# DeltaNet heads of a hybrid layer: low parts of weights and scaled value rows taken off GpSimd

## The chip, the cores and the metric

The kernel runs on one core of a Trainium2 chip, as one launch. The metric is the device time of that launch in microseconds (us), as the median of several runs; the profile is that of one more execution, whose own time stands in the table below. The engines are TensorE (PE in the profile, PEld for its weight loads), VectorE (DVE), ScalarE (ACT), GpSimd (POOL) and SyncE (SP). Each runs its own queue in order.

## What is computed

One layer for 1152 tokens (128 of context, 1024 latent) and a model width of 1024. From one normalised and modulated input h one combined projection gives q, k, v and z of four DeltaNet heads, decay and beta, the input u of a pooling mixer, and two gates. Both branches are projected, merged by the gates, projected again, and a SwiGLU layer follows. The part that the change touches, cut from the reference:

```python
def _layer(x, cvec, s0, grid_w, ...):
    h = _rmsnorm(x, g_pre_mix) * (1.0 + sc1) + sh1
    qkv, z, a, b, u, gate_a, gate_b = _split_cols(h @ w_in)
    qkv = _short_conv(qkv, conv_w)
    y_a, s_fin = _delta_branch(qkv, z, a, b, s0, a_log, dt_bias, g_onorm)
    y_b = _pool_branch(u, w_pool, pool_scale, grid_w)
    merged = jax.nn.sigmoid(gate_a) * (y_a @ w_a_proj) + jax.nn.sigmoid(gate_b) * (y_b @ w_b_proj)
...
def _gated_delta_chunked(q, k, v, g, beta, s0):
...
    t_inv = lax.linalg.triangular_solve(eye + lower, ...)
    u = jnp.einsum('nbhij,nbhjv->nbhiv', t_inv, vc * bc[..., None])
...
    def step(S, inp):
        v_new = u_i - jnp.einsum('bhck,bhkv->bhcv', w_i, S)
        o_i = jnp.einsum('bhck,bhkv->bhcv', qd_i, S) + jnp.einsum('bhij,bhjv->bhiv', intra_i, v_new)
        S = S * jnp.exp(gl_i)[..., None, None] + jnp.einsum('bhck,bhcv->bhkv', kd_i, v_new)
```

## The kernel before

**Matmuls in split form.** Each large matrix product is made of three matmuls: weight and activation are split into a high part, rounded by a copy of ACT, and a low part, source minus high part, by a `tensor_tensor` of another engine. `gemm` issues high by high (L517), high weight by low activation (L518) and low weight by high activation (L519) for each of three column chunks of 384 tokens. A weight tile comes by DMA (`wraw`); `w_split` makes `whi` (ACT, L168) and `wlo` (L169) from it, two buffers each. It is called by `w_ahead` when the first chunk of the GEMM before has done two of its steps, so the split of a weight is issued one GEMM ahead of its use. Which engine makes `wlo` stands in `lo_eng[0]`: DVE at first, POOL from the point in `gemm_stream` after the first head's q, k and v, DVE again for the layer's output projection.

**Scaled outputs.** `scaled` multiplies a PSUM result by a column, in turn on ACT (L204) and on DVE (L207, L209), and splits the product: high part on ACT (L212), low part (L214) on DVE in even turns and on `lo_alt[0]` in odd ones. `lo_alt[0]` is DVE until the normalised input is done, and POOL after it; the odd turns after it are six in `pool_proj` (the pooling mixer's group product, four groups `g` by three chunks) and four near 1003 us, in a later norm.

**The heads.** `delta_head` runs the four heads one after the other, each for both directions of the scan. Its serial chain goes: transposes of k and q (L845); products of k by k and k by q (`gk`, L873), which DVE multiplies with decay and beta into `W` and `D` (L878, L881); blocks of `W` to DRAM and back, so that 72 blocks of 32x32 stand on 72 partitions; the substitution, 31 steps of two DVE instructions each (L909 a product, L911 a sum); the result `XB` to DRAM and back as `XS` and `X`; a DVE transpose of `XS` (L952); the small matmuls `l1a` (L967) and their like, which put the 32x32 inverses together to 128x128; then nine steps of the recurrence. A `step` is PE `p1` (L1083), DVE `rr` (L1087), PE `p2` (L1097), DVE `v2` (L1102), PE `p3` (L1118), DVE `S` (L1126), with ACT's `v1` and `ou` (L1108, L1111) and the output sums `oa` (L1060, L1062, and L1064 on POOL) beside it.

**Value rows.** In the steps 14, 16 and 18 of the substitution, three blocks of v are transposed by PE into PSUM, copied to `vT` by ACT (L926) and multiplied in place by a column per block, `nk`, the reciprocal norm of k, on POOL (L927): 12 copies and 12 products in four heads.

**Order.** The program's order is written out by hand: between the serial steps the calls `fill(ns)` draw from the generator `gemm_stream` as much GEMM work (z, gates, and q, k, v of the next head) as the number asks for. All that a GEMM step issues, the weight split included, goes into the queues at that place, so an ACT copy or a low part stands between whichever rows of the serial chain were issued before and after it.

Of the kernel before, what the change touches and what calls it, by code (L numbers as in the profile page):

```python
# [12 lines left out]
AF = mybir.ActivationFunctionType  # L13
ALU = mybir.AluOpType
# [3 lines left out]
P = 128  # L18
# [5 lines left out]
CH = 384  # L24
# [55 lines left out]
def hybrid_layer(ctx: ExitStack, tc: tile.TileContext, ins, outs, dbg=None):  # L80
    nc = tc.nc
    PE, DVE, ACT, POOL, SP = nc.tensor, nc.vector, nc.scalar, nc.gpsimd, nc.sync
# [17 lines left out]
    def slot(dtype=F32, name="s"):  # L100
        uid[0] += 1
        return slots.tile([P, SL], dtype, tag="s", name=f"{name}{uid[0]}")
# [7 lines left out]
    def psd(name="d"):  # L110
        if given:
            return given.pop(0)
        uid[0] += 1
        return ps.tile([P, 512], F32, tag="d", bufs=5, name=f"{name}{uid[0]}")
# [5 lines left out]
    def v3(ap, a, b, o=0):  # L120
        return ap[:, o:o + a * b].rearrange("p (a b) -> p a b", b=b)
# [4 lines left out]
    def bc_last(ap, n):  # L126
        return ap.rearrange("p (n o) -> p n o", o=1).to_broadcast([ap.shape[0], ap.shape[1], n])
# [5 lines left out]
    lo_eng, w_dma = [DVE], [SP]  # L133
# [60 lines left out]
    lo_alt = [DVE]  # L194
# [23 lines left out]
    def sqrt_cols(x, n, inverse):  # L218

        s = small([P, 16], "rs1", 2)[:, 0:n]  # L220
        r = small([P, 16], "rs2", 2)[:, 0:n]
        a = small([P, 16], "rs3", 2)[:, 0:n]
        y = small([P, 16], "rs4", 6)[:, 0:n]
        ACT.activation(out=s, in_=x, func=AF.Sqrt)
        DVE.reciprocal(out=r, in_=s)
        DVE.tensor_tensor(out=a, in0=r, in1=r, op=ALU.mult)
        DVE.tensor_tensor(out=a, in0=a, in1=x, op=ALU.mult)
        DVE.tensor_scalar(out=a, in0=a, scalar1=-0.5, scalar2=1.5, op0=ALU.mult, op1=ALU.add)
        DVE.tensor_tensor(out=y, in0=r, in1=a, op=ALU.mult)
        if not inverse:  # L230
            z = small([P, 16], "rs5", 6)[:, 0:n]
            DVE.tensor_tensor(out=z, in0=y, in1=x, op=ALU.mult)
            return z
        return y
# [15 lines left out]
    with tc.manual_schedule():  # L250
# [112 lines left out]
        pt = psd("cs")  # L363
# [141 lines left out]
        def flush_bg():  # L505
            while bg:
                bg.popleft()()
# [65 lines left out]
        def silu_pending(n=12):  # L573
            while silus and n:
                t = silus.popleft()
                ACT.activation(out=t[:, 0:1154], in_=t[:, 0:1154], func=AF.Silu)
                n -= 1
# [91 lines left out]
        def u_task(g, early=None):  # L669
            u = slot(name="u")  # L670

            def evac(c, o):
                ACT.copy(out=u[:, c * CH:(c + 1) * CH], in_=o)

            if early is None:
                yield from gemm(8, h_at, evac)
            else:
                w, acc = early
                for c, o in enumerate(acc):
                    evac(c, o)  # L680
                w_ahead()
                w_more()
                if len(acc) < NCH:
                    yield from gemm(8, h_at, evac, w=w, chunks=range(len(acc), NCH))
            pool_group(g, u)
# [4 lines left out]
        def ab_task():  # L690

            abt.append(slot(name="ab"))
            hl, _ = w_get()
            for c in range(NCH):
                o = psg()[0:32, 0:CH]
                for k in range(8):
                    w = hl[:, k * 32:(k + 1) * 32]
                    for i, a in enumerate(h_at(k, c)):
                        PE.matmul(o, w, a, start=(k + i == 0), stop=(k + i == 8))
                    if k == 1:  # L700
                        if c == 0:
                            w_ahead()
                        elif c == 1:
                            w_more()
                    bg_tick()
                    yield 350
                ACT.copy(out=abt[0][0:32, c * CH:(c + 1) * CH], in_=o)
# [114 lines left out]
        def delta_head(h, fill, prev_final):  # L822
            def tk(t, c):
                o = tokpos(c * P)
                return t[:, o:o + P]
# [17 lines left out]
            for c in range(NT):  # L843
                pt = psd("tr")
# [26 lines left out]
            for c in range(NT):  # L871
                pt = psd("gk")
# [3 lines left out]
                cs = slice(c * P, (c + 1) * P)  # L876
                for d in range(2):
                    DVE.scalar_tensor_tensor(out=W[d][:, cs], in0=pt[:, 0:P], scalar=bn[d][:, c:c + 1],  # L878
                                             in1=IN[d][:, cs], op0=ALU.mult, op1=ALU.mult)
# [15 lines left out]
            nk = sqrt_cols(ske, NT, False)  # L895
# [6 lines left out]
            vT = slot(name="vT")  # L902
# [3 lines left out]
            for s in range(31):  # L906
                n, m = 31 - s, s + 1
                o = tt[0:72, 0:n * m].rearrange("p (r c) -> p r c", c=m)
                DVE.tensor_tensor(out=o, in0=wb[:, s + 1:32, s:s + 1].to_broadcast([72, n, m]),  # L909
                                  in1=xb[:, s:s + 1, 0:m].to_broadcast([72, n, m]), op=ALU.mult)  # L910
                DVE.tensor_tensor(out=xb[:, s + 1:32, 0:m], in0=xb[:, s + 1:32, 0:m], in1=o, op=ALU.add)  # L911
                fill(F_SUB)
                if s == 8:
                    next(prev_final, None)
                    until(f"v{h}")
                    flush_bg()
                    silu_pending()
                    vC = qkvC.pop(h)[2]
                if s in (14, 16, 18):

                    c = 3 * (s // 2 - 7)
                    cs = slice(c * P, (c + 3) * P)
                    pt = psd("tv")
                    for i in range(3):
                        PE.transpose(pt[:, i * P:(i + 1) * P], tk(vC, c + i), ident)
                    ACT.copy(out=vT[:, cs], in_=pt[:, 0:CH])  # L926
                    POOL.tensor_tensor(out=v3(vT, 3, P, c * P), in0=v3(vT, 3, P, c * P), in1=bc_last(nk[:, c:c + 3], P),  # L927
                                       op=ALU.mult)
            SP.dma_start(out=sx_d.rearrange("d c b r s -> (d c b) (r s)"), in_=XB[0:72, 0:1024])
            X = [slot(name="X") for _ in range(2)]  # L930
            Xv = [v3(x, NT, P) for x in X]
# [357 lines left out]
        def mod_ahead():  # L1289
            tiles = mod_buf.pop() if mod_buf else [slot(name="wm") for _ in range(4)]  # L1290
            mod_q.append(mod_load(*MODS[mod_i[0]], tiles))
            mod_i[0] += 1

        def mod_end():
            while mod_late:
                mod_late.pop()()
# [25 lines left out]
        def with_mod(task, ahead=True):  # L1322
            yield from task
            mod_end()
            mod_step()
            if ahead:
                mod_ahead()
            else:
                mod_buf.clear()
            yield 3000  # L1330

        def mark(name):
            done.add(name)
            return
            yield
# [3 lines left out]
        def gemm_stream():  # L1339
            mod_ahead()  # L1340
            yield from u_task(GORD[0], early[0])
            yield from u_task(GORD[1], early[1])
            for g in GORD[2:]:
                yield from with_mod(u_task(g))
            yield from with_mod(ab_task())
            yield from qkv_tasks(0, lambda t, j: with_mod(t, j < 2))
            lo_eng[0] = POOL
            yield from mark("qkv0")
            yield from pool_proj()
            mod_end()  # L1350
            for m in range(8):
                yield from yb_task(m)
            yield from mark("yb")
            for h in range(H):
                yield from z_task(h)
                yield from mark(f"z{h}")
                for i, (kind, m) in enumerate(GATES[h]):
                    if i == N_FIRST and h + 1 < H:
                        yield from qkv_tasks(h + 1)
                    if m == 7 and kind == "a":  # L1360
                        for k in range(H - 1):
                            ya_load(k)
                    yield from (ga_task if kind == "a" else gb_task)(m)
            flush_bg()
            for m in range(8):
                yield from pre_task(m)
            yield from mark("end")
# [5 lines left out]
        def fill(ns):  # L1373
            debt[0] += ns
            while debt[0] > 0 and "end" not in done:
                if stopped[0] in done:
                    debt[0] = 0.0
                    return
                x = next(stream, None)
                if x is None:  # L1380
                    break
                debt[0] -= x

        def until(name):
            while name not in done:
                next(stream, None)
# [54 lines left out]
        norm_end()  # L1441
        for i in range(len(units) - lag, len(units)):
            early_mm(*units[i])
        lo_alt[0] = POOL
        xt = None
        until("qkv0")
        fill(4000)
# [797 lines left out]
        for s, key in enumerate(keys[:-4]):  # L2245
            i, j = key[0]
# [73 lines left out]
```

## Time and profile before

| | |
|---|---|
| median of 3 runs | 1778.08 us (1776.79 to 1781.83) |
| profiled execution, its own time | 1779.98 us |
| its span | 1778.2 us |
| mean granted clock of TensorE | 0.974 of full |
| busy: PE, DVE, ACT, POOL | 1670.6, 1135.0, 712.5, 565.4 us |

The span is the time from the first to the last recorded instruction of the profiled execution; the 1.8 us between it and the execution's own time lie around it. The granted clock is the share of full speed that TensorE was allowed. DVE, ACT and POOL are busy less than two thirds of the span, so what their work costs depends on where PE waits for it.

### The profile page before, as it was taken

The page shows a single profiled execution, that of the slowest core. Times are in us where ns is not written, and L with a number is a line of the kernel's source. Part 1 is how long each engine was busy: PE and PEld are TensorE (multiplying, and loading weights), DVE is VectorE, ACT ScalarE, POOL GpSimd, SP SyncE. Part 2 cuts the span into 40 slices and gives each one's busy share as a digit, 9 for nine tenths or more (in the row PEclk, how much of TensorE's full clock was granted, in tenths as well). Part 3 has the DMA queues.
Part 4 walks back from the last instruction along what each step waited for, and adds up shares of the span by engine and source line. Part 5 has one row for each costly group of instructions (what it writes and reads, how often), then busy time and mean ns, then how long its engine had stood idle before and what let it go on. Part 6 is the DMA issues. An engine that isn't in the chain of part 4 may idle for free.

```text
span 1778.2 us, 26020 instructions
## 1 busy us (share of the span) xinstructions
PE 1670.6 (94%) x10103; PEld 1526.3 (86%) x10103; DVE 1135.0 (64%) x2067; ACT 712.5 (40%) x1381; POOL 565.4 (32%) x438
## 2 busy tenths in 40 slices
PE   5999999899999899898897799999999999899998
PEld 3977998889999889888676799999999999678776
DVE  4697546669468469457568655555555555467797
ACT  4414552463362362232356533323333333243553
POOL 0001212423333242145201456666666663000000
PEclk8999999999999899998999899999999999999999
DMA  9354432223314213453352122222222223853344
GB/s 325 99 174 156 147 113 82 67 54 114 90 32 128 57 51 122 129 203 115 107 210 98 60 92 92 93 92 92 81 79 77 84 84 113 293 203 95 126 157 172
DMA packets 173388, 211.61 MB, mean 119 GB/s; under 512 B 34956, under 2 KB 118373, under 8 KB 173265
## 3 DMA queue, kind: packets, MB, share of 16 engines
q1 hardware_dynamic: 139180, 178.35, 30.3%
q10 hardware_dynamic: 31205, 19.80, 3.8%
q0 software_dynamic: 2880, 11.80, 1.8%
q8 instruction: 79, 1.29, 0.3%
q14 instruction: 44, 0.36, 0.1%
HBM read 159.99 MB, written 49.93 MB: 118 GB/s over the span
## 4 chain that ended last, share of the span: by engine, by line
PE 46%; DVE 12%; ACT 4%; DMA 3%; issue 3%; POOL 2%; SPq 0%; DVEq 0%; ACTq 0%; POOLq 0%
PE m L1818 5%; PE m L1817 5%; PE m L1816 5%; PE dn L2160 3%; PE dn L2159 3%; PE c L1863 3%; PE dn L2158 3%; PE c L1862 3%; PE c L1861 3%; DVE WD L909 2%; PE g L517 2%; PE g L518 1%; PE g L519 1%; DVE XB L911 1%; DVE ulo L191 1%
## 5 line engine op out<-in xcount | busy, mean ns | idle before, releaser
L517 PE MATMUL g<-hh,whi 128*128 128x384 f32 x824 | 300.0, 364 | 2.8 <-ACT sga L1253 2.7
L519 PE MATMUL g<-hh,wlo 128*128 128x384 f32 x824 | 279.9, 340 | 0.0
L518 PE MATMUL g<-hl,whi 128*128 128x384 f32 x824 | 278.2, 338 | 0.0
L169 POOL TENSOR_TENSOR wlo<-wraw,whi 128x1024 fp32r<-128x1024 f32 (+2 forms) x42 | 86.3, 2055 | 280.0 <-ACT whi L168 243.6
L191 DVE TENSOR_TENSOR ulo<-wsum,uhi 128x1024 fp32r<-128x1024 f32 (+1 forms) x56 | 99.8, 1783 | 104.6 <-ACT uhi L190 104.6
L517 PEld LDWEIGHTS g<-hh,whi 128*128 128x128 f32 x824 | 156.4, 190 | 9.7 <-ACT sga L1253 3.4
L518 PEld LDWEIGHTS g<-hl,whi 128*128 128x128 f32 x824 | 157.1, 191 | 0.0
L519 PEld LDWEIGHTS g<-hh,wlo 128*128 128x128 f32 x824 | 156.0, 189 | 0.0
L1863 PE MATMUL c<-h3h,ulo 128*128 128x384 f32 x352 | 119.6, 340 | 2.7 <-DVE ulo L191 2.7
L1862 PE MATMUL c<-h3l,uhi 128*128 128x384 f32 x352 | 119.4, 339 | 0.0
L1861 PE MATMUL c<-h3h,uhi 128*128 128x384 f32 x352 | 119.2, 339 | 0.0
L1745 POOL TENSOR_TENSOR wsum<-wr,wr 128x512 f32<-128x512 f32 x63 | 101.9, 1638 | 47.8 <-DMA wr<-in_w_up_dram 43.4
L191 DVE TENSOR_TENSOR ulo<-wr,uhi 128x512 fp32r<-128x512 f32 x92 | 94.2, 1063 | 32.6 <-ACT uhi L190 32.6
L190 ACT ACTIVATE uhi<-wsum 128x1024 fp32r<-128x1024 f32 (+1 forms) x56 | 57.4, 1025 | 134.2 <-PE c L1862 50.3
L1816 PE MATMUL m<-oah,uhi 128*128 128x384 f32 x260 | 88.6, 341 | 5.7 <-ACT sgu L1828 5.7
L1745 POOL TENSOR_TENSOR wsum<-wr 128x512 f32<-128x512 f32 x43 | 58.1, 1359 | 102.5 <-DVE wlo L169 93.5
L1816 PE MATMUL m<-obh,uhi 128*128 128x384 f32 x260 | 88.8, 341 | 1.4 <-ACT uhi L190 1.4
L1818 PE MATMUL m<-obh,ulo 128*128 128x384 f32 x260 | 88.9, 342 | 0.7 <-DVE ulo L191 0.7
L2158 PE MATMUL dn<-wdhi,fh 128*128 128x512 f32 x216 | 85.8, 397 | 3.1 <-ACT fh L190 3.1
L1818 PE MATMUL m<-oah,ulo 128*128 128x384 f32 x260 | 88.6, 341 | 0.0
L1817 PE MATMUL m<-oal,uhi 128*128 128x384 f32 x260 | 88.4, 340 | 0.0
L1817 PE MATMUL m<-obl,uhi 128*128 128x384 f32 x260 | 88.4, 340 | 0.0
(448 smaller groups left out, 4419.7 us busy)
## 6 DMA issues: line engine op xcount, KB each, us to landing
wm<-in_w_mod_dram SPq DMA_DIRECT2D x48, 512.0 KB
wr<-in_w_up_dram SPq DMA_DIRECT2D x44, 512.0 KB
fr<-fo_d SPq DMA_DIRECT2D x35, 512.0 KB
wraw<-in_w_in_dram ACTq DMA_DIRECT2D x26, 512.0 KB
fo_d<-fs SPq DMA_DIRECT2D x22, 512.0 KB
wd<-in_w_down_dram SPq DMA_DIRECT2D x44, 256.0 KB
wraw<-in_w_o_dram SPq DMA_DIRECT2D x20, 512.0 KB
fo_d<-sgu SPq DMA_DIRECT2D x11, 512.0 KB
```

The source lines that it names most:

```text
L191: eng.tensor_tensor(out=lo, in0=src, in1=hi.bitcast(F32), op=ALU.subtract)
L517: PE.matmul(o, wh, a_hi, start=(k == 0), stop=False)
L518: PE.matmul(o, wh, a_lo, start=False, stop=False)
L519: PE.matmul(o, wl, a_hi, start=False, stop=(k == nk - 1))
L1745: eng.tensor_tensor(out=v3(s, 4, P, 512 * i), in0=w_block(u, a), in1=w_block(u, b), op=op)
L1816: PE.matmul(o, wh[:, ks], bh, start=(kp == 0), stop=False)
L1817: PE.matmul(o, wh[:, ks], bl, start=False, stop=False)
L1818: PE.matmul(o, wl[:, ks], bh, start=False, stop=(kp == 3))
L1861: PE.matmul(o, wh[:, ks], bh, start=(k == 0), stop=False)
L1862: PE.matmul(o, wh[:, ks], bl, start=False, stop=False)
L1863: PE.matmul(o, wl[:, ks], bh, start=False, stop=(k == 7))
L2158: PE.matmul(o, fh[:, fs], wh[:, w], start=(j == 0), stop=False)
```

## The change

Two assignments go, so that `lo_eng[0]` and `lo_alt[0]` stay DVE for the heads and `pool_proj`; and the copy and product of `vT` become three ACT activations with a scale column, one per block.

```diff
@@ delta_head, substitution, steps 14, 16 and 18
                     for i in range(3):
                         PE.transpose(pt[:, i * P:(i + 1) * P], tk(vC, c + i), ident)
-                    ACT.copy(out=vT[:, cs], in_=pt[:, 0:CH])
-                    POOL.tensor_tensor(out=v3(vT, 3, P, c * P), in0=v3(vT, 3, P, c * P), in1=bc_last(nk[:, c:c + 3], P),
-                                       op=ALU.mult)
+                    for i in range(3):
+                        ACT.activation(out=vT[:, (c + i) * P:(c + i + 1) * P], in_=pt[:, i * P:(i + 1) * P], func=AF.Copy,
+                                       scale=nk[:, c + i:c + i + 1])
@@ gemm_stream
             yield from qkv_tasks(0, lambda t, j: with_mod(t, j < 2))
-            lo_eng[0] = POOL
             yield from mark("qkv0")
             yield from pool_proj()
@@ after the normalised input
             early_mm(*units[i])
-        lo_alt[0] = POOL
         xt = None
         until("qkv0")
```

52 low parts change their engine from POOL to DVE: 42 of weights (29 of 128x1024, 8 of 128x512, 5 of 128x384) and 10 of scaled outputs (128x384). Their place in the program does not change; that of DVE's rows does, since each now stands in DVE's queue. PE's order is the same.

The first place is DVE's queue at the beginning of `pool_proj`. `ybl` and `ybh` are low and high part of an output, `sp` the scaled output itself, `wlo` a weight's low part; a row ahead of the first of these is the copy L399. Lines with + are new on DVE.

```order
+L169 TENSOR_TENSOR wlo_1508<-wraw_1329,whi_1507 128x512
+L214 TENSOR_TENSOR ybl_1514<-sp_1519,ybh_1513 128x384
 L209 TENSOR_SCALAR sp_1527<-g_1523,vcol 128x384
 L214 TENSOR_TENSOR ybl_1514<-sp_1527,ybh_1513 128x384
+L214 TENSOR_TENSOR ybl_1514<-sp_1535,ybh_1513 128x384
 L209 TENSOR_SCALAR sp_1545<-g_1541,vcol 128x384
 L214 TENSOR_TENSOR ybl_1540<-sp_1545,ybh_1539 128x384
+L214 TENSOR_TENSOR ybl_1540<-sp_1553,ybh_1539 128x384
 L209 TENSOR_SCALAR sp_1561<-g_1557,vcol 128x384
```

Between two scalings `sp` of DVE there stood one low part; now there are two, and the first of them belongs to the output that ACT has scaled.

The second place is DVE's queue in the substitution of head 0, in its second half.

```order
 L909 TENSOR_TENSOR WD_2350<-WB_2361,XB_2362 72x220
 L911 TENSOR_TENSOR XB_2362<-XB_2362,WD_2350 72x10x22
+L169 TENSOR_TENSOR wlo_2649<-wraw_2438,whi_2648 128x1024
 L909 TENSOR_TENSOR WD_2350<-WB_2361,XB_2362 72x207
 L911 TENSOR_TENSOR XB_2362<-XB_2362,WD_2350 72x9x23
```

The low part of a weight for the next head's GEMM now stands between two steps of the substitution.

The third place is DVE's queue in head 0's recurrence, between the `S` of one step and the `rr` of the next, first before the change. `qkv` (L557) is a tap of the next head's convolution.

```order
L1126 SCALAR_TENSOR_TENSOR S_3228<-S_3170,egl,p_3225 128x128
L1126 SCALAR_TENSOR_TENSOR S_3230<-S_3172,egl,p_3225 128x128
L557 SCALAR_TENSOR_TENSOR qkv_2758<-pad_151,ccol,qkv_2758 128x1154
L1087 SCALAR_TENSOR_TENSOR rr_3257<-p_3253,negc,vT_2446 128x128
L1087 SCALAR_TENSOR_TENSOR rr_3259<-p_3253,negc,vT_2446 128x128
L1102 TENSOR_SCALAR v_3269<-p_3266,bl_2246 128x128
L1102 TENSOR_SCALAR v_3271<-p_3266,bl_2252 128x128
```

And after it:

```order
L1126 SCALAR_TENSOR_TENSOR S_3231<-S_3173,egl,p_3228 128x128
L1126 SCALAR_TENSOR_TENSOR S_3233<-S_3175,egl,p_3228 128x128
L557 SCALAR_TENSOR_TENSOR qkv_2761<-pad_151,ccol,qkv_2761 128x1154
L169 TENSOR_TENSOR wlo_3248<-wraw_2807,whi_3247 128x1024
L1087 SCALAR_TENSOR_TENSOR rr_3260<-p_3256,negc,vT_2446 128x128
L1087 SCALAR_TENSOR_TENSOR rr_3262<-p_3256,negc,vT_2446 128x128
L1102 TENSOR_SCALAR v_3272<-p_3269,bl_2246 128x128
L1102 TENSOR_SCALAR v_3274<-p_3269,bl_2252 128x128
```

Between the convolution's tap and the two `rr`, for which PE's `p` (L1097) waits, a low part of 128x1024 has come in.

## Rows read from the trace of the kernel before

**Rows 1.** The page, part 1: busy us (share of the span), instructions.

```profile
PE 1670.6 (94%) x10103; PEld 1526.3 (86%) x10103; DVE 1135.0 (64%) x2067; ACT 712.5 (40%) x1381; POOL 565.4 (32%) x438
```

**Rows 2.** Waits of PE, 133 to 960 us: total us, times, longest us.

```profile
PE l1a L967 <- DVE XS L952: 12.6, 3, 5.9
...
PE p L1097 <- DVE rr L1087: 3.8, 2, 3.6
...
PE g L517 <- ACT sga L1253: 2.7, 2, 1.6
```

**Rows 3.** Groups of POOL by shape, 130 to 1000 us: busy, mean ns.

```profile
L169 POOL TENSOR_TENSOR wlo<-wraw,whi 128x1024 fp32r<-128x1024 f32 x29 | 70.5, 2432 | 190.2 <-ACT whi L168 189.9
...
L815 POOL TENSOR_TENSOR D<-D,cst 128x384 f32<-128x384 f32 x18 | 23.2, 1286 | 1.4
```

**Rows 4.** Timeline from 267.95 us: start us, us, engine, line.

```profile
268.00 0.38 DVE L909 TENSOR_TENSOR WD<-WB,XB 72x220 f32<-72x220 f32 x1
...
268.18 2.46 POOL L169 TENSOR_TENSOR wlo<-wraw,whi 128x1024 fp32r<-128x1024 f32 x1
...
268.42 2.46 DVE L911 TENSOR_TENSOR XB<-XB,WD 72x220 f32<-72x220 f32 x1
```

**Rows 5.** Timeline from 338.85 us, head 0's recurrence.

```profile
338.89 1.04 ACT L168 ACTIVATE whi<-wraw 128x1024 fp32r<-128x1024 f32 x1
...
339.43 0.61 DVE L1087 SCALAR_TENSOR_TENSOR rr<-p,negc,vT 128x128 f32<-128x128 f32 x2
...
340.02 2.38 POOL L169 TENSOR_TENSOR wlo<-wraw,whi 128x1024 fp32r<-128x1024 f32 x1 [11.74 <-ACT whi L168]
...
340.20 0.61 PE L1097 MATMUL p<-rr,X 128*128 128x128 f32 x4
...
340.85 0.61 DVE L1102 TENSOR_SCALAR v<-p,bl 128x128 f32<-128x128 f32 x2 [0.81 <-PE p L1097]
```

**Rows 6.** Four substitution loops, sums over the four windows, L909 then L911.

```profile
sum 170.00, DVE 64.25; mean DVE 16.06
...
sum 170.00, DVE 52.72; mean DVE 13.18
```

**Rows 7.** Groups of DVE by shape, 0 to 165 us.

```profile
L214 DVE TENSOR_TENSOR hl<-sp,hh 128x384 fp32r<-128x384 f32 x24 | 13.3, 555 | 11.9 <-ACT hh L212 11.8
L557 DVE SCALAR_TENSOR_TENSOR qkv<-pad,ccol,qkv 128x1154 f32<-128x1154 f32 x8 | 11.3, 1418 | 0.2
L169 DVE TENSOR_TENSOR wlo<-wraw,whi 128x1024 fp32r<-128x1024 f32 x7 | 8.5, 1220 | 2.6 <-ACT whi L168 2.6
```

**Rows 8.** Windows: length, busy PE, PEld, DVE, ACT, POOL; PEclk; DMA.

```profile
298.50:302.20 3.70, 3.70 (x64) 3.15 (x49) 1.83 (x4) 0.54 (x2) 0.00 (x0) 0.54 0.62 160
578.00:589.00 11.00, 6.46 (x155) 5.46 (x156) 5.38 (x8) 0.85 (x2) 0.00 (x0) 0.53 0.30 48
722.00:729.00 7.00, 4.74 (x82) 4.20 (x83) 3.25 (x7) 1.23 (x3) 0.00 (x0) 0.52 0.81 214
```

**Rows 9.** Groups by shape, 168 to 181 us (pool_proj).

```profile
L212 ACT ACTIVATE ybh<-sp 128x384 fp32r<-128x384 f32 x12 | 6.3, 525 | 1.7 <-DVE sp L209 1.3
...
L214 DVE TENSOR_TENSOR ybl<-sp,ybh 128x384 fp32r<-128x384 f32 x6 | 4.2, 702 | 3.5 <-ACT ybh L212 3.5
...
L209 DVE TENSOR_SCALAR sp<-g,vcol 128x384 f32<-128x384 f32 x6 | 3.6, 608 | 0.5 <-PE g L1219 0.5
L204 ACT ACTIVATE sp<-g,vcol 128x384 f32<-128x384 f32 x6 | 3.4, 572 | 0.3 <-PE g L1219 0.3
...
L557 DVE SCALAR_TENSOR_TENSOR qkv<-pad,ccol,qkv 128x1154 f32<-128x1154 f32 x1 | 2.5, 2500 | 0.0
```

**Rows 10.** Waits of DVE, 133 to 960 us.

```profile
DVE wlo L169 <- ACT whi L168: 24.8, 12, 3.7
```

**Rows 11.** Groups of ACT by shape, 160 to 800 us.

```profile
L1108 ACT ACTIVATE v<-p,bp 128x128 f32<-128x128 f32 x72 | 26.0, 366 | 78.2 <-DVE v L1102 76.1 <-PE p L1097 2.0
...
L926 ACT COPY vT<-tv 128x384 f32<-128x384 f32 x12 | 5.8, 480 | 21.8 <-PE tv L925 21.7
```

## The prediction

> **What bounds the kernel now.** The page's busy times come first: TensorE (PE) is busy for 94% of the span, VectorE (DVE) for 64%, GpSimd (POOL) for 32% [rows 1]. So no work that is moved from POOL to DVE can pay by making an engine lighter; it pays or costs where PE stands still. The change touches the stretch from 168 to 790 us, the four DeltaNet heads and a little ahead of them. There the waits of PE name what ends last [rows 2]: three of the four `l1a` matmuls wait 12.6 us in all for DVE's `XS`, the transposed result of the substitution; behind it come two waits of `p` (L1097) for `rr` of the recurrence, 3.8 us, and two of a filler GEMM for ScalarE's (ACT) `sga`, 2.7 us. All three are tails of serial chains through DVE. No row of this list is released by POOL, whose low parts of weights take 2432 ns each in their commonest shape [rows 3].
>
> The second thing to look for is a POOL row that lies beside a DVE row. At 268 us one `L911` of 72x220 takes 2.46 us, as long as the low part that POOL runs at that moment; the `L909` of the same shape just ahead took 0.38 [rows 4]. A `tensor_tensor` with both inputs in SBUF is held while POOL runs its own. In the recurrence, where DVE reads PSUM, a POOL row beside it changes nothing: two `L1102` take 0.61 us with POOL's low part running [rows 5].
>
> **What the change removes: holds in the substitution.** The 62 rows `L909`/`L911` of each head take 64.25 + 52.72 = 117.0 us over the four heads [rows 6]. The same shapes where no POOL row lies beside them (0.38 as at 268.00) add up to some 21.2 us a head, 85 in all; so 32 us are holds, by head 5.7, 8.4, 8.6 and 9.3, from 11 low parts and 12 `vT` multiplies. After the change the low parts run on DVE itself, at 1220 ns each [rows 7], as in the stretch ahead of 165 us, where DVE does this already; 2, 3, 2 and 3 of them fall in the loops (head 2's third comes behind the loop, where DVE idles), and the `vT` multiplies are gone. The loops end earlier by 5.7 − 2.4 = 3.3, 8.4 − 3.7 = 4.7, 8.6 − 2.4 = 6.2 and 9.3 − 3.7 = 5.6 us. The `l1a` stalls are 2.1, 0, 5.9 and 4.6 us. If `XS` follows the loop's end at the same distance (a store and loads by SP stand between, unchanged), no more than 0.2 is left of them: **−12.4 us**. Late next is PE's own filler work, which does not stall. Bounds: 0, if the transfers alone set `XS`, and −12.6.
>
> **The clock behind these stalls.** [...] Work at half speed could be done in half its busy time: 3.7/2, 6.46/2 and 4.74/2, together 1.9 + 3.2 + 2.4 = 7.5 us. Part of the first PE work there is thin and might be slow anyway, so I take **−6**, bounds 0 and −7.5.
>
> **What it adds: pool_proj, 168 to 181 us.** Each output is scaled by ACT (`L204`, 572 ns) in odd turns and by DVE (`L209`, 608) in even ones, then ACT writes its high part (`L212`, 525) and POOL or DVE its low part [rows 9]. Before, a pair costs ACT 0.57 + 2 x 0.525 = 1.62 us, with DVE and POOL beside it (1.68 from start to start). After, the odd low part stands on DVE ahead of the next even `L209`, as the first piece of the order shows, and the chain is serial: ACT 0.57, ACT 0.525, DVE 0.55 [rows 7], DVE 0.61, ACT 0.525, which is 2.7 with the handovers that lie under one another. That is +1.0 a pair, and for the fifth pair's low part, the first that the next GEMM reads (`yb`), +4.3, less the 0.9 for which it lies ready now: +3.4 or a little more. Behind it DVE has four convolution taps (`L557`), the softplus chain and two weights' low parts in their midst, of which the second comes 1.9 us late in the same counting. Sum **+5.4**, bounds +4 and +7. The other low parts up to 255 us fall where DVE has nothing to do: 0.
>
> **gk and W, heads 1 to 3.** One low part of each head falls between `L878` and `L881`, on the chain that goes over `W`, the square roots and ACT's table load to the `sga` that PE waits for [rows 2]. Each lengthens it by nearly its 1.22: 3 x 1.15 = **+3.5**; bounds 0 (if another input than this chain ends last) and +3.7.
>
> **The recurrence.** Fifteen low parts come between its serial steps. I followed each: when its high part is ready, when DVE comes to it, and how long PE's next matmul can wait. The last piece of the order is one of them: the high part ends at 339.93, so DVE holds `rr` back from 339.43 to about 341.17; the first `rr` ends 1.74 us later than its 339.78, and `p` (L1097, at 340.20) had 0.42 to spare: +1.3 [rows 5]. Seven others give 0 (the five of 128x384 among them), the rest +0.3, +0.7, +0.7, +0.8, +1.4 and +1.85, and one −0.5, since POOL's `oa` no longer queues behind a low part. **+6.5**, bounds +3 and +13: where DVE makes low parts already, 12 of them wait 24.8 us for their high parts, 2.1 on the mean, 3.7 at the worst [rows 10]; a wait of DVE is one of whatever stands behind it, and in the recurrence that is what PE's next step reads.
>
> **vT on ACT.** Three rows of 128x128 out of PSUM with a scale column, 366 ns each, for one copy of 480 [rows 11]: at most +0.62 us, twelve times. They stand in the substitution, where ACT waits for PE's transposes and PE has filler work: 0 on the path, and up to +0.62 each if a transpose's PSUM buffer were waited for. The low parts of `o_norm` at 1003 us: 0, within 0.5. A new stretch at the lower clock in pool_proj: **+1** (0 to 3).
>
> **Sum.** −12.4 − 6 + 5.4 + 3.5 + 6.5 + 1 = −2.0 us. The profiled execution took 1779.98 us, so 1778.0; the median of the runs is 1778.08, 1.9 below it, so 1776.1 there. I forecast **1776**: no change that can be told, on the faster side. A difference of 0.3%, or 5.3 us, is about what a measurement here can tell from none.
>
> [...] What the trace shows is the hold, 2.46 us in place of 0.38 [rows 4]. [...] But the moved low parts have two SBUF inputs themselves, so they stay open to holds by what POOL still runs. By the trace alone this is the third rival below.
>
> **Rivals.** *Faster* (0.27): the clock comes back whole (−7.5), pool_proj costs its lower bound (+4) and the recurrence its own (+3), no new low clock: −12.4 − 7.5 + 4 + 3.5 + 3 = −9.4, so 1768.7. For it speaks that the `l1a` waits are PE's largest; against it, that the low parts that I followed in the recurrence do wait for their high parts.
>
> *Slower, by low parts ahead of serial steps* (0.18): in the recurrence DVE comes to a low part before its high part is there, and holds `rr`, `v2` or `S` for the wait too. If seven of them cost 1.22 + 2.1 − 0.4 = 2.9 us each [rows 7, 10], they are 20 us in place of 6.5: 1789.6. It decides from 2.0 us a low part (14 in place of 6.5; the sum is then +5.5). For it speaks the one of 1.85; against it, that ACT's queue gives the high parts at the same places as now.
>
> *POOL's remaining rows hold the moved low parts* (0.15): `L815` (1286 ns) and its like stay on POOL in the recurrence [rows 3]; a low part on DVE that meets one takes up to 1.2 us longer, as an `L557` took 2500 ns beside POOL's work in pool_proj [rows 9] against 1418 [rows 7]. Four such meetings in series are +5: 1781. For it: such meetings exist now, with `L557`; against it: POOL's queue is emptier after the change, and its rows run earlier.
>
> **How the numbers follow.** The forecast itself holds 0.40, of which 0.27 within 0.3%, 0.09 faster, 0.04 slower. The faster rival gives 0.25 faster and 0.02 the same; the slower one 0.17 and 0.01 the same; the third 0.01 faster, 0.08 the same, 0.06 slower. Together: faster 0.35, the same 0.38, slower 0.27. The likeliest's own range is 1771 to 1781; that for 8 in 10 reaches into both sides, 1767 to 1787.
>
> **What would show it.** Right: `L909` and `L911` near 21 us a head, `l1a` with no wait for `XS`, and a clock of 1.00 after it; PE waiting some 5 us more before 200 us; new waits of `p` for `rr` and `v2` of about 1 us each, and longer ones for `sga`. Wrong: `l1a` still waiting, for the loads of `XS`; waits in the recurrence of over 2 us; new half-clock stretches behind them. One such stretch of 10 us would move the sum by 5, more than the sum itself.

## The result and the profile after

The changed kernel takes 1786.79 us (median of 9 runs, 1782.24 to 1791.64) against 1776.79 (9 runs, 1773.05 to 1781.83) of the kernel before: a ratio of 1.0052, with a 95% interval of 1.0039 to 1.0065. It is slower, by some 9 us; no change, on the faster side, had been forecast.

The two profiled executions are not a fair pair by their totals. That of after took 1782.24 us, the fastest of its nine; that of before 1779.98, 3.2 above its own median. They are 2.3 us apart where the medians are 10. What makes them comparable is that PE runs the same 10103 instructions in the same order in both (some 40 of the smallest matmuls exchange places within 0.1 us), so the start of each can be set against its start in the other. Counted so, after stands at −1.9 us at 160 us (ahead of the change), at +3.3 at 200 us, and at +5.9 at 801 us: 7.8 us are lost in the stretch that the change touches. Behind it, where both kernels are the same, after wins 5.3 us back by 1040 us, with a granted clock of 0.94 from 801 to 1040 us against 0.92, and loses 1.7 of them later. That is scatter, and it hides most of the loss in the spans.

The page of after, its first part: busy time, share and instructions of each engine.

```profile
PE 1667.0 (94%) x10103; PEld 1522.0 (85%) x10103; DVE 1142.8 (64%) x2119; ACT 717.3 (40%) x1405; POOL 457.9 (26%) x374
```

POOL has lost a fifth of its work, DVE is as busy as before, PE too; the answer to [rows 1] tells nothing of the loss. The waits of PE from 133 to 975 us do (total us, times, longest):

```profile
PE p L1097 <- DVE rr L1087: 10.1, 6, 3.6
...
PE g L517 <- ACT sga L1253: 5.0, 2, 2.8
...
PE p L1083 <- DVE S L1126: 3.2, 2, 2.2
PE g L1217 <- DVE sp L209: 2.8, 4, 0.9
PE gk L873 <- DVE D L881: 1.8, 3, 0.8
PE p L1118 <- DVE v L1102: 1.8, 2, 1.1
...
PE l1a L967 <- DVE XS L952: 1.5, 2, 1.2
PE g L519 <- issue: 1.3, 1, 1.3
```

Against [rows 2], `l1a` has fallen from 12.6 to 1.5 us, as forecast. In its place stand six waits for `rr` in place of two, longer ones for `sga`, `S`, `sp` and `D`, and two new ones for `v2` (`v`, L1102). The substitution loops of the four heads, `L909` and then `L911`, sums over four windows that hold the whole loops:

```profile
sum 167.00, DVE 43.60; mean DVE 10.90
...
sum 167.00, DVE 42.10; mean DVE 10.52
```

85.7 us in place of the 117.0 of [rows 6], by head 21.0, 21.5, 21.6 and 21.6: the holds are gone. The clock, in windows (length, busy PE, PEld, DVE, ACT, POOL; granted clock; DMA):

```profile
179.00:187.00 8.00, 8.00 (x35) 8.00 (x35) 5.90 (x12) 5.62 (x10) 0.00 (x0) 0.57 0.01 2
298.50:305.00 6.50, 6.50 (x157) 5.38 (x161) 2.74 (x7) 1.44 (x5) 0.00 (x0) 1.00 0.43 107
326.00:331.00 5.00, 5.00 (x26) 4.99 (x26) 1.70 (x6) 3.86 (x8) 4.74 (x7) 0.66 0.56 143
405.00:409.00 4.00, 3.67 (x12) 3.67 (x13) 2.59 (x6) 2.10 (x4) 2.56 (x2) 0.57 1.05 305
552.00:556.00 4.00, 4.00 (x15) 4.00 (x15) 3.01 (x9) 1.56 (x3) 2.02 (x2) 0.57 0.94 296
590.00:601.00 11.00, 9.44 (x230) 7.43 (x229) 4.55 (x10) 4.33 (x8) 0.00 (x0) 1.00 0.12 17
627.00:631.00 4.00, 4.00 (x18) 4.00 (x17) 1.86 (x7) 2.43 (x5) 1.39 (x2) 0.57 0.02 4
728.00:736.00 8.00, 7.18 (x173) 5.98 (x171) 4.25 (x8) 1.23 (x3) 0.00 (x0) 1.00 0.87 296
```

Behind the three `l1a` places (298.5, 590, 728) the clock is now 1.00 where [rows 8] showed 0.52 to 0.54. But there are stretches at a lower level (0.50 of full inside one, as from 183 to 186 us) at 179, 326, 405, 552 and 627, all but the first where the clock was 1.00 before. Those at 405, 552 and 627 stand directly behind the longer `sga` waits of heads 1 and 2 and the `rr` wait of 2.3 us in head 2. Not every such wait has one: behind two other added waits of 2.2 us, at 369 us (`rr`) and at 515 us (`S`), the clock stays at 1.00 (windows 369 to 373 and 515 to 519).

### The profile page after: what moved, and what is told of

It reads as the page before. It is cut to its first block, busy times and chain, and to the rows that moved or that the text cites. A ratio compares the mean times of both kernels' runs of the same rounds, so it can differ in the third digit from the quotient of the medians.

```text
span 1780.4 us, 26002 instructions
## 1 busy us (share of the span) xinstructions
PE 1667.0 (94%) x10103; PEld 1522.0 (85%) x10103; DVE 1142.8 (64%) x2119; ACT 717.3 (40%) x1405; POOL 457.9 (26%) x374
## 3 DMA queue, kind: packets, MB, share of 16 engines
q8 instruction: 79, 1.29, 0.3%
## 4 chain that ended last, share of the span: by engine, by line
PE 54%; DVE 9%; ACT 5%; issue 3%; POOL 2%; DMA 1%; SPq 0%; ACTq 0%; DVEq 0%; POOLq 0%
PE m L1816 5%; PE m L1815 5%; PE m L1814 5%; PE dn L2158 4%; PE dn L2156 4%; PE dn L2157 4%; PE g L517 3%; PE c L1861 3%; PE c L1859 3%; PE c L1860 3%; PE g L519 3%; PE g L518 3%; DVE wlo L169 1%; PE o L1548 1%; DVE ulo L191 1%
## 5 line engine op out<-in xcount | busy, mean ns | idle before, releaser
L519 PE MATMUL g<-hh,wlo 128*128 128x384 f32 x824 | 280.7, 341 | 1.3 <-issue 1.3
L519 PEld LDWEIGHTS g<-hh,wlo 128*128 128x128 f32 x824 | 156.5, 190 | 1.6 <-issue 1.6
L169 DVE TENSOR_TENSOR wlo<-wraw,whi 128x1024 fp32r<-128x1024 f32 (+2 forms) x73 | 81.8, 1121 | 80.5 <-ACT whi L168 80.3
L2158 PE MATMUL dn<-wdhi,fl 128*128 128x512 f32 x216 | 86.3, 399 | 1.9 <-DVE fl L191 1.9
```

The costliest lines, as they stand in the source:

```text
L519: PE.matmul(o, wl, a_hi, start=False, stop=(k == nk - 1))
L2158: PE.matmul(o, fl[:, fs], wh[:, w], start=False, stop=(j == NJ - 1))
```

## Experiments

Ratios are to the kernel before, timed beside each on the same chip; the intervals are of 95%. A line number in a changed kernel is that of the profile of that kernel.

**e1: the value rows alone.** The kernel before with only the first hunk of the change (ACT scales `vT`); both assignments to POOL stay.

> The kernel before with only the value rows changed: ACT scales them out of PSUM, all low parts stay on POOL. Theory A (the change loses by low parts that stand ahead of serial steps on DVE, and by half-clock stretches behind those waits; it gains by the holds that go from the substitution): the three vT holds of each loop go (0.5 to 0.9 us each, more where a vT queued behind a low part), the l1a waits fall from 12.6 to about 6, and nothing is added: 3 to 7 us faster than before, about 1772. Rival B (the extra ACT rows cost): slower than before by 1 to 5 us. Rival C (the transfers set XS, so the holds do not count): the same within 2 us, l1a waits still about 12.

1772.44 us, ratio 0.9981 (0.9969 to 0.9993). The wait of `l1a`:

```profile
PE l1a L967 <- DVE XS L952: 8.0, 3, 5.0
```

12.6 has become 8.0. The holds by the `vT` products did lie on the path, and ACT's extra rows (368 ns each in the profile after) cost nothing that outweighs it.

**e2: low parts on DVE in the substitution alone.**

```diff
+            lo_eng[0] = DVE
             for s in range(31):
...
             silu_pending(1)
             DVE.transpose(out=XTbv, in_=XDv[1])
+            lo_eng[0] = POOL
```

> The kernel before with the value rows on ACT, and the weights' low parts on DVE only from the first step of each head's substitution to the transposes of XS; POOL elsewhere, pool_proj included. Theory A: the gain of the substitution without the costs elsewhere: l1a waits fall from 12.6 to under 2 and the half-clock stretches behind them go, 12 to 18 us faster than before, about 1762. Rival B (the rows on ACT, or DVE in the loop, cost as much as they give): 1774 to 1782. Rival C: the same as before within 2 us, l1a still waiting about 12.

1766.93 us, ratio 0.9945 (0.9927 to 0.9963). Some of PE's waits:

```profile
PE p L1099 <- DVE rr L1089: 4.1, 2, 3.6
...
PE g L519 <- issue: 2.2, 1, 2.2
...
PE l1a L969 <- DVE XS L954: 1.4, 2, 1.1
```

`l1a` waits 1.4 us, `rr` as before. This is the gain without the costs: about 10 us, and 20 us below the changed kernel. It fell short of the 12 to 18 expected; one new wait of 2.2 us, for which the profile names no releaser, takes part of it.

**e3: the opposite.** The changed kernel with POOL in the substitution and DVE everywhere else: the two lines of e2 the other way round.

> The changed kernel with the low parts back on POOL from the first step of each substitution to the transposes of XS; on DVE everywhere else. Theory A: the costs without most of the gain: l1a waits come back to about 6 us, with a half-clock stretch or two behind them; 5 to 10 us slower than the changed kernel, 14 to 19 slower than before, about 1793. Rival C: the same as the changed kernel, some 9 us over before. Rival D (the low parts on DVE in the loop are themselves what costs): faster than the changed kernel, about 1778.

1793.53 us, ratio 1.0095 (1.0077 to 1.0113).

```profile
PE p L1099 <- DVE rr L1089: 10.6, 6, 3.6
PE l1a L969 <- DVE XS L954: 5.6, 3, 2.6
...
PE g L517 <- ACT sga L1255: 5.0, 2, 2.8
```

The new waits of `rr` and `sga` are the changed kernel's, and 5.6 us of `l1a` are back. e2 and e3 divide the change: some 10 us gained by what goes from the loops, and 17 lost by the low parts elsewhere, even with the value rows on ACT.

**e4: POOL up to the first head.** The changed kernel with both removed assignments put back, and this ahead of the heads:

```diff
+        lo_eng[0] = lo_alt[0] = DVE
         final = iter(())
         for h in range(H):
```

> The changed kernel with all moved low parts back on POOL up to the first head (pool_proj, gate preparation, decay), on DVE from the first head on. Theory A: PE is no longer 5 us late at 200 us, and nothing later gives this back: 5 us faster than the changed kernel, 4 slower than before, about 1781. Rival E (the lateness at 200 us is hidden later, as heads wait for transfers or ACT): the same as the changed kernel within 2 us.

1783.62 us, ratio 1.0036 (1.0018 to 1.0054): by the times some 3 us of the changed kernel's 10 are pool_proj's, with intervals that overlap. The trace is clearer: from 160 to 240 us PE loses nothing against the kernel before, where the changed kernel loses 5.2 us. The medians give back less, with the clock's scatter between.

**e5 and e6: POOL in the recurrence, POOL in the products gk.** The changed kernel, in e5 with `lo_eng[0] = POOL` from the transposes of `XS` to the end of the recurrence, in e6 during the `gk` loop; DVE elsewhere.

> The changed kernel with the low parts back on POOL from the transposes of XS to the end of each head's recurrence; DVE elsewhere. Theory A (low parts ahead of serial steps on DVE cost PE their length less the slack, and call forth half-clock stretches): the waits of p for rr, S and v2 that the change added go (about 7 us), with two stretches of 1.7 us behind them: 8 to 11 us faster than the changed kernel, about 1777. Rival F (what is lost in the recurrence is DVE's load, given back by shorter waits later): 0 to 3 us faster, about 1785.

> The changed kernel with the low parts back on POOL during the products gk (from the first gk matmul to the last W) of each head; DVE elsewhere. Theory A: three low parts leave the chain to sga; waits of PE for sga fall from 5.0 to about 2.7, those for D and jk by some 1 to 2, and the half-clock stretches behind the sga waits (at 405 and 552 us) go: 4 to 7 us faster than the changed kernel, about 1781. Rival F: the same as the changed kernel within 2 us.

e5: 1776.30 us, ratio 0.9998 (0.9982 to 1.0014), so the recurrence is worth 10 us, as expected. e6: 1782.55, ratio 1.0034 (1.0019 to 1.0049), so the gk phases are worth 3 to 4, at the lower end of what was expected or below it; here the interval overlaps that of the changed kernel. The waits are plainer: in e6 `sga` waits 2.7 us, as in [rows 2], and the stretches at the lower clock behind the `sga` waits are gone; in e5 `rr` waits 3.8, as there.

**e7: e2 without the new value rows.** The kernel before with only e2's two lines; `vT` is copied by ACT and multiplied by POOL.

> As the kernel that kept DVE's low parts to the substitution (e2), but with the value rows as in the kernel before: ACT's copy and POOL's product. Theory A: each head's loop has three short holds again, 0.5 us each, since the products no longer queue behind a low part: the loops end 1.5 us later than in e2, l1a waits 1 to 2 us more: 1 to 3 us slower than e2, 7 to 9 faster than before, about 1769. Rival G (the value rows carry most of e2's gain): 1773 or more.

1762.85 us, ratio 0.9931 (0.9906 to 0.9957). It had been expected 1 to 3 us slower than e2, and came out 4 us faster by the medians and 2.5 by the ratios. The intervals overlap, so only this follows: once no low part stands in POOL's queue in the loops, moving the value rows brings nothing that can be measured.

**e8: is it DVE, or the place in its queue?** As e4, but with a low part's instruction held back in the program while its high part is made where it was.

```diff
-        lo_eng[0].tensor_tensor(out=lo[:, 0:n], in0=t[:, 0:n], in1=hi[:, 0:n].bitcast(F32), op=ALU.subtract)
+        pend.append((lo[:, 0:n], t[:, 0:n], hi[:, 0:n].bitcast(F32)))
+        if not held[0]:
+            lo_flush()
...
                 late_o()
+                lo_flush()
                 for d in range(2):
```

`held[0]` is set from a head's transposes of k to those of `W` (where `lo_flush` issues what is held), and through the recurrence (where each step issues it behind `v2` and the output sums). `w_more`, the load of the next raw weight, waits for the flush.

> All low parts of the heads on DVE as in the changed kernel, POOL only up to the first head as in e4; but inside the products gk and the recurrence a low part's instruction is held back in the program: behind the transposes of W in the first case, behind the scaled v2 and the output sums in the second, where DVE waits for PE anyway. Theory A (it is the place in DVE's queue that costs, not the engine): most of the recurrence's 7 us and the 4.5 us of the gk phases go, with the half-clock stretches behind them: 1764 to 1770, as e2. Rival H (DVE's work costs wherever it stands): 1779 to 1784, as e4.

1774.49 us, ratio 0.9981 (0.9964 to 0.9997): 9 us better than e4, but not the 1764 to 1770 of theory A. Two of PE's waits, and a row of ACT's timeline:

```profile
PE g L535 <- DVE wlo L179: 4.3, 1, 4.3
...
PE g L533 <- DVE sg L1266: 2.2, 1, 2.2
...
668.41 1.28 ACT L240 ACT_TABLE_LOAD   x1 [2.18 <-DVE wlo L179]
```

Holding back made waits of its own. In head 0 a low part was held until a GEMM stood waiting for it. In head 3 the load of the next raw weight stood in ACT's queue directly behind the flush, needed the low part to be done, and held ACT's table load for 2.18 us.

**e9: the same, mended.** No holding back in head 0 ahead of its recurrence, and in the other heads from the products on, not from the transposes of k; the load is issued later than the low part (behind the squares of the step, or ahead of the value rows).

> As e8, with two waits mended that holding back had made there: no holding back in head 0 ahead of its recurrence, and the load of the next raw weight, which stands in ACT's queue and needs the low part done, is issued later than the low part. Theory A (the place in DVE's queue costs, not the engine): the waits of 4.3 us for a low part at 251 us and of 2.1 at 675 go, and with them 6 of e8's 1774.5 us: 1765 to 1770. Rival H (DVE's load costs): 1773 or more.

1764.59 us, ratio 0.9930 (0.9908 to 0.9951), at the edge of what was expected. The same low parts are on DVE here as in e4, which is 19 us slower. The timeline of DVE in head 0's recurrence:

```profile
335.30 0.61 DVE L1111 SCALAR_TENSOR_TENSOR rr<-p,negc,vT 128x128 f32<-128x128 f32 x2
336.72 0.61 DVE L1126 TENSOR_SCALAR v<-p,bl 128x128 f32<-128x128 f32 x2 [0.81 <-PE p L1121]
337.24 0.48 DVE L1084 TENSOR_TENSOR oa<-p,ou 128x128 f32<-128x128 f32 x2
337.64 1.22 DVE L179 TENSOR_TENSOR wlo<-wraw,whi 128x1024 fp32r<-128x1024 f32 x1
338.77 0.60 DVE L1152 SCALAR_TENSOR_TENSOR S<-S,egl,p 128x128 f32<-128x128 f32 x2
```

The low part (1.22 us) now lies between the output sums and `S`; `rr` and `v2` are where they would be without it, and PE's waits for `S` are those of the kernel before (1.5 us in two). Two of PE's waits:

```profile
PE p L1121 <- DVE rr L1111: 4.0, 2, 3.8
...
PE g L536 <- ACT sga L1282: 1.7, 1, 1.7
```

**e10 and e11: the best of it.** The kernel before with low parts on DVE in the substitution, and in the recurrence held back as in e9; POOL in the gk phases and ahead of the heads. In e10 ACT scales the value rows, in e11 POOL does.

> Low parts on DVE in the substitution, as in e2, and in the recurrence too, there held back behind v2 and the output sums as in e9; on POOL in the products gk and ahead of the heads. Value rows on ACT. Theory A: e2's time less the wait of p for v of 1.8 us in head 2, since POOL's sum no longer queues behind a low part, and less what the convolution taps are held now: 1 to 4 us faster than e2, about 1763. Rival H: 1768 or more.

> As e10, with the value rows as in the kernel before, copied by ACT and multiplied by POOL. Theory A, with what e7 showed (the value rows are worth less than the clock's scatter once no low part is in POOL's queue): the same as e10 within 3 us. Rival G (ACT's three rows cost more than the copy): 3 to 5 us faster than e10.

e10: 1764.48 us, ratio 0.9926 (0.9905 to 0.9948). e11: 1764.15, ratio 0.9929 (0.9908 to 0.9950). Both beat both kernels; neither beats e7 or e9 by anything that can be told. The value rows make no difference here either.

**e12: the disputed cost by itself.** The kernel before with rows on DVE that nobody needs:

```diff
+                    if h < 3 and cf in (3, 5):
+                        dz = small([P, CH], "sp", 4)
+                        for _ in range(8):
+                            DVE.tensor_copy(out=dz, in_=kC[:, 0:CH])
                     for d in range(2):
                         c = cc[d]
                         r[d] = small([P, P], "rr", 3)
```

> The kernel before with eight added DVE copies of 128x384 (about 0.3 us each, 2.4 together, one SBUF input, result unused) ahead of rr in steps 3 and 5 of heads 0 to 2, six places; nothing is moved. Priced as a low part there would be, by length less DVE's idle time and PE's slack of 0.1 to 0.7 us, they make PE wait some 1.9 us a place, 11.6 in all. Theory A with the clock's part: some of these waits are followed by a half-clock stretch of 3.4 us, which costs 1.7: 12 to 20 us slower than before. Rival I (later waits give the delays back): under 6 slower.

1810.58 us, ratio 1.0181 (1.0157 to 1.0205): 32 us, above the 12 to 20 expected. Two things made up the difference. The copies took longer than thought, eight of them 3.1 us in the three quiet places, and in the other three they met POOL. One of those, in the timeline, with the wait of PE behind it:

```profile
634.39 6.83 DVE L1087 COPY sp<-qkv 128x384 f32<-128x384 f32 x8
...
635.65 2.48 POOL L169 TENSOR_TENSOR wlo<-wraw,whi 128x1024 fp32r<-128x1024 f32 x1 [5.16 <-ACT whi L168]
...
641.14 0.60 DVE L1091 SCALAR_TENSOR_TENSOR rr<-p,negc,vT 128x128 f32<-128x128 f32 x2
...
641.63 1.20 PE L1101 MATMUL p<-rr,X 128*128 128x128 f32 x4 [6.13 <-DVE rr L1091]
```

And all waits of that kind:

```profile
PE p L1101 <- DVE rr L1091: 26.5, 8, 6.1
```

22.7 us more than the 3.8 of [rows 2]. The rule of price (length less idle time and slack) holds for the lengths that came out: 11.6, and 6 x 0.7 = 4.2 for the longer copies, and holds of 2.5, 1.5 and 3.7 us make 23.5. The remaining 9 us of the 32 are put down to the clock; in the two profiled executions, which drift 35 us apart from 290 to 801 us, its part is 14. Between 290 and 800 us the lower level is granted in twelve separate stretches where [rows 8] has its three, and `l1a` waits 12.1 us as before. Each of the six added waits has one of the twelve within 1.3 us of its end; two of them (columns as in [rows 8]), behind waits that end at 353.9 and 506.1 us:

```profile
353.70:357.70 4.00, 3.82 (x17) 3.85 (x18) 1.85 (x7) 1.14 (x4) 0.00 (x0) 0.57 0.00 0
...
507.00:511.00 4.00, 4.00 (x18) 4.00 (x17) 1.45 (x6) 3.48 (x6) 0.00 (x0) 0.57 0.00 0
```

Waits that are added, with nothing moved, call them forth.

## Why the prediction was wrong

PE's start times give each term of the sum its measured counterpart, over 160 to 800 us (steps at one instruction are waits, the slow drift between them is the clock):

| term | predicted | in the profiles |
|---|---|---|
| `l1a` waits | −12.4 | −11.2 |
| clock, stretches behind `l1a` | −6 | −5.6 |
| clock, new stretches | +1 | +8.0 |
| pool_proj and early, waits | +5.4 | +3.3 |
| gk and W | +3.5 | +4.7 |
| recurrence | +6.5 | +7.3 |
| `g` L519 behind `l1a` | 0 | +1.5 |
| the rest, no piece over 0.7 | 0 | −0.2 |
| sum | −2.0 | +7.8 |

**The step that failed is the term for new stretches at the lower clock: "+1 (0 to 3)", in pool_proj alone.** It measured +8.0. The other half of the clock was right: the stretches behind the `l1a` waits did go, and gave back 5.6 us where −6 had been taken, from the busy time of PE and the clock in the three windows of [rows 8] (0.50 inside them, as over 300 to 302, 585 to 588 and 725 to 727 us). But five new or longer ones came, at 180, 326, 405, 552 and 627 us, 1.6 us each by PE's starts. That is 7.0 of the 9.8 us between the two sums. The prediction priced the waits that go together with the clock behind them, and those that come in the products and the recurrence without it, as if it cost nothing there; it named such stretches only among the signs of being wrong. Four of the five stand where the change added to a wait; that at 326 us stands behind a wait that the kernel before has too. By the windows above, each of the new stretches at 326, 405, 552 and 627 costs some 1.7 us (405 to 409: 4 us at 0.57, so 4 x 0.43), and that at 179 to 187 costs 8 x 0.43 = 3.4, twice that of the kernel before at this place. e12 shows it alone: waits added, nothing moved, and 9 of 32 us in the clock, 14 by its profile. e5 agrees: the recurrence's 7.3 us of waits were worth 10 in the time.

**The substitution** went as argued for the holds: 85.7 us against an unheld 85, and e2 and e3 show its worth from both sides. The loops of heads 0, 2 and 3 end earlier by 3.5, 5.3 and 6.2 us, where 3.3, 6.2 and 5.6 had been forecast. That of head 1 does not (34.5 us from first row to last, 34.3 before; 4.7 less had been forecast), since a low part in it waits 2.74 us for its high part at 437 us, among other waits. This cost nothing only because PE does not wait for that loop: its `l1a` stalls 0 us before and 0.3 after. What was late next was not nothing, however: at 736 us a GEMM's L519 waits 1.29 us for something that the profile does not name, in the middle of the 32x32 matmuls.

**pool_proj** became the serial chain that was read from the order. Its timeline after:

```profile
168.92 0.61 DVE L209 TENSOR_SCALAR sp<-g,vcol 128x384 f32<-128x384 f32 x1
169.56 0.52 ACT L212 ACTIVATE ybh<-sp 128x384 fp32r<-128x384 f32 x1 [1.15 <-DVE sp L209]
...
169.59 0.45 PE L1217 MATMUL g<-dh,whi 128*128 128x384 f32 x1 [0.78 <-DVE sp L209]
...
170.00 0.56 ACT L204 ACTIVATE sp<-g,vcol 128x384 f32<-128x384 f32 x1
...
170.59 0.52 ACT L212 ACTIVATE ybh<-sp 128x384 fp32r<-128x384 f32 x1
...
171.15 0.56 DVE L214 TENSOR_TENSOR ybl<-sp,ybh 128x384 fp32r<-128x384 f32 x1 [0.47 <-ACT ybh L212]
171.62 0.61 DVE L209 TENSOR_SCALAR sp<-g,vcol 128x384 f32<-128x384 f32 x1
```

From `L209` to `L209` it is 2.70 us, as worked out, and PE's L1217 waits for each `sp`. The further 1.9 us for a late weight did not come as a wait; 1.7 of clock came in its place, so the total of 5.2 us stands near the 5.4 by an accident.

**gk and the recurrence** were priced by length less slack. The three places in gk came out at 3.2 us against 3.5. In the recurrence 7.3 stands near 6.5 partly by luck: seven places cost 9.9 us where 7.05 had been priced, and shorter waits gave back 2.6 where 0.5 had been. Most of that is one wait in head 2, in the kernel before:

```profile
PE p L1053 <- ACT v L1108: 1.8, 1, 1.8
```

It is gone in the changed kernel, and back in e5. Head 0's low part in the transposes of k, priced at 0, cost 1.4 in waits for `jk` and `D`. The place that was worked out ahead, at 339 us, came out so:

```profile
341.73 1.04 ACT L168 ACTIVATE whi<-wraw 128x1024 fp32r<-128x1024 f32 x1
...
342.80 1.23 DVE L169 TENSOR_TENSOR wlo<-wraw,whi 128x1024 fp32r<-128x1024 f32 x1 [0.61 <-ACT whi L168]
...
343.94 0.60 DVE L1087 SCALAR_TENSOR_TENSOR rr<-p,negc,vT 128x128 f32<-128x128 f32 x2
...
344.43 0.68 PE L1097 MATMUL p<-rr,X 128*128 128x128 f32 x4 [1.23 <-DVE rr L1087]
```

The high part ends at 342.77, the low part holds `rr` to 343.94, and PE waits 1.23 us; +1.3 had been forecast.

**The rivals.** "Slower, by low parts ahead of serial steps" had the mechanism and the sign, though not the price: its waits for high parts of 2.1 us each did not come (in the recurrence they are 0.4 to 1.0 us, and 1.7 once), and the clock made up for them. That POOL's remaining rows would hold the moved low parts is refuted in the main, by the mean of these from 130 to 1000 us:

```profile
L169 DVE TENSOR_TENSOR wlo<-wraw,whi 128x1024 fp32r<-128x1024 f32 x50 | 63.0, 1261 | 61.2 <-ACT whi L168 61.2
```

1261 ns against the 1220 of [rows 7], 2 us over fifty of them, of which 1.4 lie in two rows behind the heads. In the heads one is longer, beside POOL's `L814` and `L815`, and it did lie on the path:

```profile
623.97 1.78 DVE L169 TENSOR_TENSOR wlo<-wraw,whi 128x1024 fp32r<-128x1024 f32 x1 [0.97 <-ACT whi L168]
```

It makes some 0.55 us of PE's wait of 2.3 us for `rr` at 626 us. "Faster" failed with the step above: the clock came back nearly whole, but not without new stretches.

**What stays open:** the wait without a releaser near the 32x32 matmuls of head 3. In the changed kernel it is this row:

```profile
736.47 0.45 PE L519 MATMUL g<-hh,wlo 128*128 128x384 f32 x1 [1.29 <-issue]
```

It is 1.3 to 2.7 us in the changed kernel and in eight experiments that have `l1a` early in that head (e2, e4, e5, e6 and e8 to e11), 0.4 in e1, and absent from the kernel before, e3 and e12, where `l1a` waits there; but e7, with `l1a` early, has none there. The traces do point somewhere. The page lists a DMA queue of kind "instruction", q8: 79 packets and 1.29 MB in the changed kernel, some 16 KB each. One such transfer begins at 734.01 us in the changed kernel, 2.46 us before PE goes on, and this is its row for 733.9 to 734.95 us:

```profile
q8 instruction: 1, 0.02, 5.5%
```

In all nine kernels with the wait, and for the 0.4 us of e1, PE goes on 2.3 to 2.5 us after such a transfer began. So PE may have waited for its own instructions, of which the 32x32 matmuls use up many in a short time (PE runs 74 matmuls in these 1.05 us): in this place the next transfer follows after 3.5 us, elsewhere mostly after some 20. No run changes this, so the cause is argued, not shown.

## What to carry to other kernels

A helper instruction that is given to an engine in a serial chain costs by its place in that engine's queue: the same low parts made this kernel 9 us slower where they were issued with their weights, and, with POOL kept ahead of the heads, 12 us faster (e9) where they were issued behind a row after which the engine waits anyway. Where an engine's holds on another are the trouble, move the work only in the stretch where the holds are on the path (e2, e7), and leave it elsewhere. When waits are added and removed, price both with the clock that follows them (−5.6 and +8.0 us here), or neither.

## What the runs showed of the hardware

A DVE copy with one SBUF input was held beside POOL as well. In e12 eight copies of 128x384 took 3.1 us where POOL was quiet, and 6.83 us from 634.39 us, where POOL ran a low part of 2.48 us and rows of `L814` and `L815`; all 48 took 25.0 us. The prediction had given the hold to a `tensor_tensor` with both inputs in SBUF.

In these runs the stretches at the lower clock moved about with the waits that precede them. A wait of PE of 3.6 us at 324 us stood in the kernel before without one behind it [rows 2] (1.00 over 324 to 331 us); in the changed kernel the same wait has one, at 326 to 331 us (0.66). A price for the clock behind a single wait is therefore a chance, not a number, and executions of one kernel differ by several us with it: of the 19 runs of the kernel before that stand beside e1 to e4, the three slowest (1780.5 to 1785.3 us) have a mean granted clock of 0.971, the two fastest (1770.3 and 1770.7) 0.979 and 0.981.
